# The second product of the last FFN: VectorE's emptying of a shared accumulator placed ahead of the splits, and two weight sums placed two steps later

## The chip, the core and the metric

The kernel runs on one core of one Trainium2 chip. A core has a matrix engine (TensorE, PE in the profile), which multiplies and adds into accumulators in PSUM, and three engines that work on vectors: VectorE (DVE), ScalarE (ACT) and GpSimd (POOL). Each engine carries out its own queue of instructions in order; semaphores let an instruction of one queue wait for another queue's. SyncE (SP) and GpSimd issue transfers here. The metric is the device time of one execution in microseconds (us), the median of several runs.

## The reference, cut to what matters

The program is a two-layer trunk over 512 tokens of width 1024, in float32. Each layer is a token mixer and a dense SwiGLU block, each with a norm before and after it. The change lies in the last SwiGLU block, in its second product (`@ w_out`, 512 x 2816 by 2816 x 1024), and so in the last 120 us of the program:

```python
def swiglu_ffn(h, w_in, w_out):
    gate, up = jnp.split(h @ w_in, 2, axis=-1)
    return (jax.nn.silu(gate) * up) @ w_out
...
        h = rmsnorm(x, norm_g[i, 2]) * (1.0 + scale) + shift
        y = swiglu_ffn(h, f_w_in[i], f_w_out[i])
        x = x + gate * rmsnorm(y, norm_g[i, 3])
```

## The kernel before

**Precision.** Every float32 operand of a matmul is split in two: ScalarE copies it into a rounded "high" half and VectorE subtracts that from the operand to get the "low" half. A product is then three matmuls: high by high, low weight by high, high by low activation (L1788). So every tile that TensorE reads has cost one ScalarE copy and one VectorE subtraction.

**Seven products in place of eight.** The 512 x 2816 activations and the 2816 x 1024 weights are cut into 2 x 2 blocks, and the four blocks of the result are made from seven block products (`PRODUCTS`), whose operands are sums and differences of blocks. The inner dimension is gone through in `NP` = 11 pairs `p` of 128-row blocks. Products 0 to 3 add into accumulators A, B, C and D; products 4, 5 and 6 add on into A. Each accumulator is two PSUM tiles, one for each half of 128 tokens: `bank["A"][0]` and `bank["A"][1]`, in the profile both `cA`.

**A is read three times on the way.** It is never restarted, so its value has to be taken out between products: after product 0 it is copied (the result block `got["11"]`, with B added later), after product 4 it is subtracted from C + D (`got["12"]`, L2018), after product 5 from D (`got["22"]`, L2020), and after product 6 it is the last block itself. TensorE may not add the next product's first step into a half of A before that half has been read.

**Parts.** The 77 steps (product, pair) are grouped into 40 parts of one or two steps. TensorE goes through them in order: the first token half of the part, then the second. A part of two steps is 12 matmuls, one of one step 6. Product 4 ends with part 27 (one step), product 5 is parts 28 to 33 (33 has one step), product 6 is parts 34 to 39.

**The order of the engines' queues** is the order of the code here: this stretch is recorded without the scheduler on all five engines. The loop over `n` (L2045) records, for each part, its matmuls (`products`), then the vector work due behind it (`behind`), then the splits of the weights of part n+4 (`w_prep`, L1754 on ScalarE and L1755 on VectorE, tile `whlo`, four buffers) and of the activations of part n+3 (`a_prep`, L1767 and L1768, tile `ao`, three buffers). Below, "w30" and "a29" are the splits for the weights of part 30 and the activations of part 29. With these buffer counts w30 waits for TensorE's part 26, and a29 for the same part. From part 34 on, `behind` comes after the splits.

**What `behind` does.** At n = 27 and 33 it empties A with two VectorE instructions, one per token half. At n = 29 and 30 ScalarE squares result blocks for the closing norm and VectorE forms a mean (L1983, L1986). From n = 34 on come the roots, the gates (L1993) and the sums into the output rows (L1999). `t3(p)` (L1801) is VectorE's weight sum for product 5: block 22 minus block 11 of pair p, in place. One is due at each n from 17 to 27; the sums of pairs 9 and 10, at n = 26 and 27, are read by ScalarE's copies w32 and w33.

Of the kernel before, what the change touches and what calls it, by code (L numbers as in the profile page):

```python
# [35 lines left out]
def trunk_kernel(  # L36
# [26 lines left out]
    def t2(name):  # L63
        return tmp.tile([P, T], F32, tag="t2", name=name, bufs=4)
# [985 lines left out]
    with ExitStack() as ph:  # L1050
# [99 lines left out]
        class Group:  # L1150
# [169 lines left out]
            def root(self):  # L1320
                self.rg = t2("rg")
                act.activation(self.rg, self.ssg, AF.Sqrt, bias=eps_t, scale=1.0 / 256)
# [219 lines left out]
    with ExitStack() as ph:  # L1542
# [4 lines left out]
        NP = NF // 2  # L1547
# [28 lines left out]
        def b_(i, name, q=None):  # L1576

            t = rows_of[i][int(name[1]) - 1][:, :, slice(0, T) if name[2] == "1" else slice(T, D)]
            return t if q is None else t[:, q, :]
# [156 lines left out]
        turns = [odd if i in (1, 3) else even for i in range(7)]  # L1736
# [7 lines left out]
        def w_prep(n):  # L1744
            w = whl_p.tile([P, 2, 2, T], F32R, tag="whl", name="whlo")
            part = parts[n]
            us = {unit_of[p] for _, p in part}
            if len(us) == 1 and len(part) == 2:
                todo = [(slice(0, 2), b_(us.pop(), PRODUCTS[part[0][0]][1]))]
            else:  # L1750
                todo = [(slice(q, q + 1), b_(unit_of[p], PRODUCTS[i][1])[:, units[unit_of[p]].index(p):][:, :1])
                        for q, (i, p) in enumerate(part)]
            for sl, srcw in todo:
                act.copy(w[:, 0, sl, :], srcw)  # L1754
                dve.tensor_tensor(w[:, 1, sl, :], srcw, w[:, 0, sl, :].bitcast(F32), SUB)  # L1755
            w_of[n] = w

        def a_prep(n):
            a = fo.tile([P, 2, 2, 256], F32R, tag="ao", name="ao")
            part = parts[n]  # L1760
            if len(part) == 2 and part[0][0] == part[1][0] and part[1][1] == part[0][1] + 1:
                todo = [(slice(0, 2), part[0], 2)]
            else:
                todo = [(slice(q, q + 1), st, 1) for q, st in enumerate(part)]
            for sl, (i, p), m in todo:
                srca = a_(PRODUCTS[i][2], p, m)
                act.copy(a[:, 0, sl, :], srca)  # L1767
                dve.tensor_tensor(a[:, 1, sl, :], srca, a[:, 0, sl, :].bitcast(F32), SUB)  # L1768
            for _, (i, p), m in todo:
                if i == 0:  # L1770
                    dve.tensor_tensor(a_("a11", p, m), a_("s1", p, m), a_("a11", p, m), SUB)
                elif i == 1:
                    dve.tensor_add(a_("a12", p, m), a_("a12", p, m), a_("a11", p, m))
            a_of[n] = a
# [3 lines left out]
        def products(tiles):  # L1778
            for sub in range(2):
                for n in tiles:  # L1780
                    for q, (i, p) in enumerate(parts[n]):
                        r = PRODUCTS[i][0]
                        if r not in bank:
                            bank[r] = [(mm_ps if r == "C" else aux_ps)(f"c{r}{t}") for t in range(2)]
                        first = i == {"A": 0, "B": 1, "C": 2, "D": 3}[r] and p == turns[i][0]
                        last = p == turns[i][-1]
                        w, a, tk = w_of[n], a_of[n], slice(sub * P, (sub + 1) * P)
                        for k, (hl, al) in enumerate(((0, 0), (1, 0), (0, 1))):  # L1788
                            pe.matmul(bank[r][sub], a[:, al, q, tk], w[:, hl, q, :],  # L1789
                                      start=first and k == 0, stop=last and k == 2, skip_group_check=True)  # L1790

        with tc.manual_schedule(engines={PE_ENGINE, mybir.EngineType.SP, mybir.EngineType.Activation,
# [5 lines left out]
            def t3(p):  # L1798
                i = unit_of[p]
                q = units[i].index(p)  # L1800
                dve.tensor_tensor(b_(i, "b11", q), b_(i, "b22", q), b_(i, "b11", q), SUB)  # L1801

            def t2_(i):
                add_(b_(i, "b22"), b_(i, "b12"))

            def t4(i):
                add_(b_(i, "b21"), b_(i, "b22"))
# [174 lines left out]
            def square(t, part, src):  # L1982
                act.activation(spare["junk"], src, AF.Square, accum_out=st[t]["s2"][:, part:part + 1])  # L1983

            def mean(t):
                dve.tensor_scalar(st[t]["b1"], st[t]["s2"][:, 0:1], 1.0 / D, EPS, MUL, ADD)  # L1986
# [5 lines left out]
            def gated(src, hf, dst):  # L1992
                dve.tensor_mul(dst, src, gg[hf])  # L1993
                return dst

            def x_new(t, hf, yg, parts=(FULL,), puts=(dma,)):
                for c, put in zip(parts, puts):
                    cx = slice(hf * T + c.start, hf * T + c.stop)
                    dve.scalar_tensor_tensor(xt[t][:, cx], yg[:, c], st[t]["s1"], xt[t][:, cx], MUL, ADD)  # L1999
                    put(out[0, t * P:(t + 1) * P, cx], xt[t][:, cx])  # L2000

            def behind(n):

                for t in range(2):
                    if n == 5:
                        got["11", t] = t2("c11")
                        act.copy(got["11", t], bank["A"][t])
                    elif n == 10:
                        dve.tensor_add(got["11", t], got["11", t], bank["B"][t])
                    elif n == 16:  # L2010
                        got["12", t] = t2("c12")
                        act.copy(got["12", t], bank["C"][t])
                    elif n == 21:
                        dve.tensor_add(got["12", t], got["12", t], bank["D"][t])
                        got["22", t] = spare[f"c22_{t}"]
                        act.copy(got["22", t], bank["D"][t])
                    elif n == 27:
                        dve.tensor_tensor(got["12", t], got["12", t], bank["A"][t], SUB)  # L2018
                    elif n == 33:
                        dve.tensor_tensor(got["22", t], got["22", t], bank["A"][t], SUB)  # L2020
                    elif n in (29, 30):
                        if t == n - 29:
                            square(t, 0, got["11", t])
                            square(t, 1, got["12", t])
                            mean(t)
                    elif n == 34:
                        root(t)
                        gated(got["11", t], 0, got["11", t])
                    elif n == 35:
                        square(2 + t, 0, got["22", t])  # L2030
                        mean(2 + t)
                        gated(got["12", t], 1, got["12", t])
                        x_new(t, 0, got["11", t])
                    elif n == 36:
                        gated(got["22", t], 1, got["22", t])
                        x_new(t, 1, got["12", t])
                for i, u in enumerate(units):
                    if n == 8 + u[-1] // 2:
                        t2_(i)
                    if n == 19 + i:  # L2040
                        t4(i)
                if 17 <= n < 17 + NP:
                    t3(turns[5][n - 17])

            for n in range(NT - 3):  # L2045
                products([n])
                if n < 34:
                    behind(n)
                if n == 26:
                    for hf in range(2):  # L2050
                        dma(gg[hf], gate_d[3, 4 * hf:4 * hf + 4].rearrange("j p -> (j p)").partition_broadcast(P))
                if n + 4 < NT:
                    w_prep(n + 4)
                if n + 3 < NT:
                    a_prep(n + 3)
                if n >= 34:
                    behind(n)
# [40 lines left out]
```

## Time and profile before

| what | us |
|---|---|
| median of 3 runs | 1345.12 |
| lowest, highest run | 1344.85, 1346.7 |
| the profiled execution's own time | 1345.17 |
| its span, first to last instruction | 1343.0 |
| TensorE idle between parts 27 and 28 | 2.02 |
| TensorE idle between parts 33 and 34 | 1.97 |
| TensorE idle ahead of part 39's last matmul of the first half | 0.39 |

The span is what the trace covers; the profiled execution's own time holds 2.2 us more around it. The parts of the changed stretch are read from the timeline, in us from the span's start: product 4 begins at 1286.26, product 5 at 1303.40, product 6 at 1320.60, and TensorE's last matmul ends at 1336.52. The mean granted TensorE clock is 0.999 of full speed. Matmuls overlap: the length of a group of them is not the sum of their single lengths. A wait is put down to one releaser, the one that came last by the profile.

### The profile page before, as it was taken

How to read it: one execution, taken by the hardware profiler on the slowest of the kernel's cores; microseconds unless marked ns; L12 is line 12 of the kernel's file. 1: busy time of each engine (PE TensorE's matmuls, PEld its weight loads, DVE VectorE, ACT ScalarE, POOL GpSimd, SP SyncE). 2: the span in 40 equal slices, each digit the busy share in tenths (PEclk: the TensorE clock that was granted, in tenths of full speed). 3: DMA queues.
4: the chain of work that ended last, by engine and by line, in shares of the span. 5: the costliest groups of instructions: out<-in, count | busy, mean ns of one | idle time of the engine just before them, and what ended most of it. 6: DMA issues, size and time to landing. Idle time of an engine off the chain costs nothing.

```text
span 1343.0 us, 19136 instructions
## 1 busy us (share of the span) xinstructions
PE 1326.6 (99%) x7485; PEld 1143.8 (85%) x7485; DVE 985.2 (73%) x1581; ACT 618.2 (46%) x995; POOL 65.3 (5%) x82
## 2 busy tenths in 40 slices
PE   8999999999999999999999999999999999999997
PEld 7788889888888888898888888888889999998875
DVE  5588866778787322659889988888677777767887
ACT  5323356222323211665644555554474555544664
POOL 0000000000000000000000000000000111101320
PEclk9999999999999999999999999999999999999999
DMA  9757760777776322513543344423251788779851
GB/s 311 237 179 233 252 206 1 225 245 234 238 247 221 126 94 67 157 33 118 165 130 114 91 128 124 132 73 125 79 157 46 192 219 210 199 200 286 166 108 63
DMA packets 199886, 215.90 MB, mean 161 GB/s; under 512 B 8292, under 2 KB 148468, under 8 KB 198772
## 3 DMA queue, kind: packets, MB, share of 16 engines
q1 hardware_dynamic: 186384, 184.74, 44.3%
q0 software_dynamic: 9264, 17.04, 7.4%
q10 hardware_dynamic: 4148, 12.90, 3.0%
q8 instruction: 59, 0.97, 0.3%
q14 instruction: 31, 0.25, 0.1%
HBM read 195.37 MB, written 2.24 MB: 147 GB/s over the span
## 4 chain that ended last, share of the span: by engine, by line
PE 91%; issue 3%; DMA 2%; ACT 2%; DVE 1%; SPq 0%; DVEq 0%; ACTq 0%; POOLq 0%
PE ip L276 14%; PE ip L278 14%; PE ip L277 14%; PE sA L1694 6%; PE y L378 6%; PE y L380 6%; PE y L379 6%; PE cA L1789 4%; PE sC L1694 3%; PE li L756 2%; PE li L276 2%; PE li L277 2%; PE li L278 2%; PE sB L1694 2%; PE yd L1283 1%
## 5 line engine op out<-in xcount | busy, mean ns | idle before, releaser
L276 PE MATMUL ip<-h,whl 128*128 128x512 f32 x840 | 331.2, 394 | 0.2 <-DVE cv L863 0.2
L278 PE MATMUL ip<-h,whl 128*128 128x512 f32 x840 | 327.2, 390 | 0.0
L277 PE MATMUL ip<-h,whl 128*128 128x512 f32 x840 | 327.0, 389 | 0.0
L276 PEld LDWEIGHTS ip<-h,whl 128*128 128x128 f32 x840 | 157.8, 188 | 33.8 <-issue 1.8
L278 PEld LDWEIGHTS ip<-h,whl 128*128 128x128 f32 x840 | 157.7, 188 | 33.4
L277 PEld LDWEIGHTS ip<-h,whl 128*128 128x128 f32 x840 | 157.8, 188 | 31.6
L222 DVE TENSOR_TENSOR whl<-wst,whl 128x1024 fp32r<-128x1024 f32 x99 | 120.4, 1221 | 60.1 <-ACT whl L221 59.9
L124 DVE SCALAR_TENSOR_TENSOR ada_acc<-ada_st,csil,ada_acc 128x512 f32<-128x512 f32 x140 | 105.0, 750 | 3.9 <-DMA ada_st<-in_ada_w_dram 0.4
L204 DVE TENSOR_TENSOR whlo<-wsto,whlo 128x1024 fp32r<-128x1024 f32 x41 | 49.9, 1224 | 78.2 <-ACT whlo L203 78.0
L221 ACT CAST whl<-wst 128x1024 fp32r<-128x1024 f32 x99 | 103.0, 1041 | 3.2 <-DMA wst<-in_a_w_in_dram 1.8
L276 PE MATMUL li<-h,whl 128*128 128x256 f32 x288 | 83.2, 289 | 0.0
L278 PE MATMUL li<-h,whl 128*128 128x256 f32 x288 | 81.6, 283 | 0.0
L277 PE MATMUL li<-h,whl 128*128 128x256 f32 x288 | 81.5, 283 | 0.0
L203 ACT CAST whlo<-wsto 128x1024 fp32r<-128x1024 f32 x41 | 42.6, 1050 | 76.4 <-PE y L380 75.0
L1694 PE MATMUL sA<-tq,whl 128*128 128x256 f32 x576 | 74.6, 283 | 0.3 <-DVE g L1720 0.3
L1694 PEld LDWEIGHTS sA<-tq,whl 128*128 128x128 f32 x576 | 71.6, 192 | 0.6 <-DVE g L1720 0.5
L378 PE MATMUL y<-whlo,ff 128*128 128x512 f32 x176 | 68.6, 390 | 0.0
L380 PE MATMUL y<-whlo,ff 128*128 128x512 f32 x176 | 68.5, 389 | 0.0
L379 PE MATMUL y<-whlo,ff 128*128 128x512 f32 x176 | 68.5, 389 | 0.0
L1142 DVE SCALAR_TENSOR_TENSOR cu<-ip,cols,cu 128x511 f32<-128x511 f32 (+2 forms) x84 | 62.8, 747 | 3.9 <-ACT cu L1139 1.4
L1789 PE MATMUL cA<-whlo,ao 128*128 128x512 f32 x264 | 61.2, 390 | 4.4 <-ACT ao L1767 4.0
L1789 PEld LDWEIGHTS cA<-whlo,ao 128*128 128x128 f32 x264 | 49.3, 188 | 15.7 <-ACT ao L1767 4.8
(328 smaller groups left out, 2436.0 us busy)
## 6 DMA issues: line engine op xcount, KB each, us to landing
ada_st<-in_ada_w_dram SPq DMA_DIRECT2D x96, 512.0 KB, 5.2
wst<-in_f_w_in_dram SPq DMA_DIRECT2D x26, 1024.0 KB, 6.5
wst<-in_m_w_in_dram SPq DMA_DIRECT2D x14, 1024.0 KB, 5.4
wsto<-in_f_w_out_dram SPq DMA_DIRECT2D x10, 1024.0 KB, 5.1
wst<-in_m_w_in_dram SPq DMA_DIRECT2D x20, 512.0 KB, 5.2
wst<-in_a_w_in_dram SPq DMA_DIRECT2D x9, 1024.0 KB, 5.9
wsu<-in_f_w_in_dram SPq DMA_DIRECT2D x17, 512.0 KB, 5.8
csb<-cs_d ACTq DMA_DIRECT2D x8, 1024.0 KB, 5.2
```

The source lines that it names most:

```text
L124: dve.scalar_tensor_tensor(acc, w, csil[:, k:k + 1], acc, MUL, ADD)
L221: later.append((lambda sw=sw, w=w: act.copy(w[:, 0, :nk, :], sw), lambda sw=sw, w=w: dve.tensor_tensor(w[:, 1, :nk, :], sw, w[:, 0, :nk, : ...
L222: lambda sw=sw, w=w: dve.tensor_tensor(w[:, 1, :nk, :], sw, w[:, 0, :nk, :].bitcast(F32), SUB)))
L276: pe.matmul(dst, w_at(w, 0, kk), a[:, 0, sl], start=start, stop=False)
L277: pe.matmul(dst, w_at(w, 0, kk), a[:, 1, sl], start=False, stop=False)
L278: pe.matmul(dst, w_at(w, 1, kk), a[:, 0, sl], start=False, stop=stop)
L378: pe.matmul(pst, a[:, 0, tk], wt[:, 0, kk, :], start=k == 0, stop=False)
L379: pe.matmul(pst, a[:, 0, tk], wt[:, 1, kk, :], start=False, stop=False)
L380: pe.matmul(pst, a[:, 1, tk], wt[:, 0, kk, :], start=False, stop=k == K - 1)
L1142: dve.scalar_tensor_tensor(u[:, sft:], pst[:, :T - sft], w[3 - sft], u[:, sft:], MUL, ADD)
L1694: pe.matmul(dst, w[:, wl, k0 + k, :], moving(q, k, al), skip_group_check=True, start=q in ("P1", "P5", "P2") and k == 0 and i == 0, stop=k ...
L1789: pe.matmul(bank[r][sub], a[:, al, q, tk], w[:, hl, q, :], start=first and k == 0, stop=last and k == 2, skip_group_check=True)
```

## The change

Two edits in the code that records this stretch.

- The loop no longer records part 27 in its own turn. At n = 26 it records part 26, its `behind`, then part 27 and `behind(27)`, and only then w30 and a29. In the same way parts 32 and 33 are recorded together, with `behind(33)` ahead of w36 and a35. TensorE's order of matmuls is the same as before.
- A table gives the weight sums that are due: none at n = 26 and 27, pair 9 at n = 28 and pair 10 at n = 29.

```diff
-                if 17 <= n < 17 + NP:
-                    t3(turns[5][n - 17])
+                for p in {26: (), 27: (), 28: (NP - 2,), 29: (NP - 1,)}.get(n, (n - 17,)):
+                    if 0 <= p < NP:
+                        t3(turns[5][p])
 
             for n in range(NT - 3):
-                products([n])
-                if n < 34:
+                if n not in (27, 33):
+                    products([n])
+                if n in (26, 32):
+                    behind(n)
+                    products([n + 1])
+                    behind(n + 1)
+                elif n < 34 and n not in (27, 33):
                     behind(n)
                 if n == 26:
```

VectorE's queue around the first emptying, as a piece of the difference. The first row is the low half of a28; L1801 is a weight sum, the three rows below the added pair are w30 (two) and a29, the rows at the end belong to w31:

```order
 L1768 TENSOR_TENSOR ao<-raw,ao 128x512
-L1801 TENSOR_TENSOR w2h_10839<-w2h_10840,w2h_10839 128x512
+L2018 TENSOR_TENSOR c_11258<-c_11258,cA_10902 128x512
+L2018 TENSOR_TENSOR c_11260<-c_11260,cA_10903 128x512
 L1755 TENSOR_TENSOR whlo<-w2t_10664,whlo 128x512
 L1755 TENSOR_TENSOR whlo<-w2s,whlo 128x512
 L1768 TENSOR_TENSOR ao<-raw,ao 128x512
-L2018 TENSOR_TENSOR c_11258<-c_11258,cA_10902 128x512
-L2018 TENSOR_TENSOR c_11260<-c_11260,cA_10903 128x512
-L1801 TENSOR_TENSOR w2h_10841<-w2h_10842,w2h_10841 128x512
 L1755 TENSOR_TENSOR whlo<-w2s,whlo 128x512
```

Four instructions that stood between a28 and the emptying stand behind it or further back, and the second sum leaves its place behind the emptying.

The two sums come back further down the same queue; the first row is a30's low half, then w32 (two), a31, a mean, w33:

```order
 L1768 TENSOR_TENSOR ao<-raw,ao 128x512
+L1801 TENSOR_TENSOR w2h_10839<-w2h_10840,w2h_10839 128x512
 L1755 TENSOR_TENSOR whlo<-w2h_10837,whlo 128x512
 L1755 TENSOR_TENSOR whlo<-w2h_10839,whlo 128x512
 L1768 TENSOR_TENSOR ao<-raw,ao 128x512
 L1986 TENSOR_SCALAR ss<-ss 128x1
+L1801 TENSOR_TENSOR w2h_10841<-w2h_10842,w2h_10841 128x512
 L1755 TENSOR_TENSOR whlo<-w2h_10841,whlo 128x512
```

Each sum now stands directly ahead of the splits that use its result (`w2h_10839` in w32, `w2h_10841` in w33).

VectorE's queue around the second emptying; the first two rows are w35 and a34, the rows after the added pair w36 (two) and a35, the last one w37:

```order
 L1755 TENSOR_TENSOR whlo<-w2t_10756,whlo 128x1024
 L1768 TENSOR_TENSOR ao<-raw,ao 128x512
+L2020 TENSOR_TENSOR w2h_10839<-w2h_10839,cA_10902 128x512
+L2020 TENSOR_TENSOR w2h_10841<-w2h_10841,cA_10903 128x512
 L1755 TENSOR_TENSOR whlo<-w2t_10664,whlo 128x512
 L1755 TENSOR_TENSOR whlo<-w2s,whlo 128x512
 L1768 TENSOR_TENSOR ao<-raw,ao 128x512
-L2020 TENSOR_TENSOR w2h_10839<-w2h_10839,cA_10902 128x512
-L2020 TENSOR_TENSOR w2h_10841<-w2h_10841,cA_10903 128x512
 L1755 TENSOR_TENSOR whlo<-w2s,whlo 128x512
```

Three splits that stood ahead of the pair stand behind it.

## The prediction

> **What bounds the kernel now.** I read the page's first part for the bound, then the list of waits for what TensorE (PE) waits for, then the timeline of each engine over the last 60 us, where the change lies. Columns of a timeline row: start in us, length in us, engine, line, operation, out<-in, count, and in brackets the idle time ahead of the row with what ended it.
>
> ```profile
> span 1343.0 us, 19136 instructions
> ...
> PE 1326.6 (99%) x7485; PEld 1143.8 (85%) x7485; DVE 985.2 (73%) x1581; ACT 618.2 (46%) x995; POOL 65.3 (5%) x82
> ...
> PE cA L1789 <- ACT ao L1767: 4.0, 2, 2.0
> ```
>
> TensorE is busy 99% of the span, so only its gaps can be won. The largest entry in its list of waits is the 4.0 us, in two waits, on the accumulator `cA` of the last product. They stand in TensorE's timeline:
>
> ```profile
> 1286.26 15.12 PE L1789 MATMUL cA<-whlo,ao 128*128 128x512 f32 x66
> 1303.40 15.22 PE L1789 MATMUL cA<-whlo,ao 128*128 128x512 f32 x66 [2.02 <-ACT ao L1767]
> 1320.60 11.61 PE L1789 MATMUL cA<-whlo,ao 128*128 128x512 f32 x50 [1.97 <-ACT ao L1767]
> 1332.60 3.92 PE L1789 MATMUL cA<-whlo,ao 128*128 128x512 f32 x16 [0.39 <-DVE ao L1768]
> ```
>
> Each x66 group is one product (11 pairs, 2 token halves, 3 matmuls), so a matmul is issued every (15.12-0.39)/65 = 0.227 us. TensorE stands still between parts 27 and 28 and between 33 and 34. The view blames a ScalarE copy into `ao`. VectorE (DVE) and ScalarE (ACT) at the first gap tell another story:
>
> ```profile
> 1298.42 1.23 DVE L1755 TENSOR_TENSOR whlo<-w2t,whlo 128x1024 fp32r<-128x1024 f32 x1 [0.56 <-ACT whlo L1754]
> 1299.57 0.69 DVE L1768 TENSOR_TENSOR ao<-raw,ao 128x512 fp32r<-128x512 f32 x1
> ...
> 1300.17 0.68 DVE L1801 TENSOR_TENSOR w2h<-w2h,w2h 128x512 f32<-128x512 f32 x1
> 1300.77 0.68 DVE L1755 TENSOR_TENSOR whlo<-w2t,whlo 128x512 fp32r<-128x512 f32 x1
> 1301.37 0.68 DVE L1755 TENSOR_TENSOR whlo<-w2s,whlo 128x512 fp32r<-128x512 f32 x1
> 1301.97 0.68 DVE L1768 TENSOR_TENSOR ao<-raw,ao 128x512 fp32r<-128x512 f32 x1
> 1302.58 1.28 DVE L2018 TENSOR_TENSOR c<-c,cA 128x512 f32<-128x512 f32 x2
> ...
> 1302.66 0.61 ACT L1767 CAST ao<-raw 128x512 fp32r<-128x512 f32 x1
> ```
>
> The `ao` copy at 1302.66 is the high half for part 30, which TensorE does not need for part 28. What part 28 needs is `cA` emptied: the first instruction of the L2018 pair ends at 1302.58+0.68 = 1303.26, and TensorE starts 0.14 us later, ahead of the pair's end at 1303.86: each token half is released by its own eviction. VectorE was never idle here. It did four instructions, 0.60 us apart, ahead of the eviction: a weight sum (L1801) and three splits for parts 30 and 29. The second gap has the same picture, without a sum:
>
> ```profile
> 1316.81 0.69 DVE L1768 TENSOR_TENSOR ao<-raw,ao 128x512 fp32r<-128x512 f32 x1
> ...
> 1317.96 0.69 DVE L1755 TENSOR_TENSOR whlo<-w2t,whlo 128x512 fp32r<-128x512 f32 x1 [0.46 <-ACT whlo L1754]
> ...
> 1319.78 1.28 DVE L2020 TENSOR_TENSOR w2h<-w2h,cA 128x512 f32<-128x512 f32 x2
> ```
>
> 1319.78+0.68+0.14 = 1320.60, TensorE's restart.
>
> **The first eviction moved.** Nothing is removed or added; VectorE's rows change places. With the sum and the splits gone from ahead of it, VectorE is free at 1300.17 and waits for the first half of `cA` alone. That this half is enough is seen at an earlier eviction, which began before the accumulator's last matmul ended (1286.42):
>
> ```profile
> 1271.98 14.44 PE L1789 MATMUL cD<-whlo,ao 128*128 128x512 f32 x63
> ...
> 1286.26 1.28 DVE L2014 TENSOR_TENSOR c<-c,cD 128x512 f32<-128x512 f32 x2
> ```
>
> Part 27 has six matmuls, three to a half. The half's last one is the first of these four:
>
> ```profile
> 1300.31 1.07 PE L1789 MATMUL cA<-whlo,ao 128*128 128x512 f32 x4
> ...
> 1317.33 1.29 PE L1789 MATMUL cA<-whlo,ao 128*128 128x512 f32 x5
> ```
>
> It ends at 1300.31+0.39 = 1300.70. How long VectorE takes to follow a matmul's end I bound by two rows: ScalarE follows TensorE's 1332.60+3.92 = 1336.52 at 1336.56 (0.04), and VectorE follows 1185.87+1.60 = 1187.47 at 1187.58 (0.11):
>
> ```profile
> 1185.87 1.60 PE L1694 MATMUL sB<-h,whl 128*128 128x256 f32 x12
> ...
> 1187.58 0.42 DVE L1707 TENSOR_TENSOR g<-sB,g 128x256 f32<-128x256 f32 x1 [1.05 <-PE sB L1694]
> ...
> 1336.56 0.60 ACT L1983 ACTIVATE w2s<-cA 128x512 f32<-128x512 f32 x1 [2.35 <-PE cA L1789]
> ```
>
> With 0.08: eviction at 1300.78, done at 1301.46, TensorE on at 1301.60 instead of 1303.40. **Gain 1.80** (1.77 to 1.84). A gap of 0.22 remains, since the last three matmuls of part 27 cover most of the eviction. The second half's eviction ends by 1302.2; TensorE reaches that half six matmuls (1.36) after 1301.60, at 1302.96.
>
> [...]
>
> **What is now late behind it.** The three splits come after both evictions: the low half of part 29's `ao` starts four places behind 1300.78, at about 1303.26, and is there at 1303.95 instead of 1302.65. TensorE wants it with the third matmul of part 29: 1301.60 + 2.72 (12 matmuls) + 0.45 = 1304.77, so 0.7 us of cover. If it were gone, a late split would cost TensorE its lateness once.
>
> **The two weight sums.** Each is 0.68 us on VectorE, not on TensorE's path, but ScalarE's copies for parts 32 and 33 read their results. Behind the evictions stand w30 (two), a29, w31 (two), a30, six at 0.60, so the first sum runs 1305.66 to 1306.34 and ScalarE's second w32 copy starts at 1306.38. Before, it began 0.52 into the first pair here (a mean, L1986, on VectorE stands among ScalarE's rows):
>
> ```profile
> 1306.42 1.14 ACT L1754 CAST whlo<-w2h 128x512 fp32r<-128x512 f32 x2 [3.15 <-PE cA L1789]
> ...
> 1307.99 0.63 ACT L1983 ACTIVATE w2s<-c 128x512 f32<-128x512 f32 x1
> ...
> 1308.74 0.63 ACT L1983 ACTIVATE w2s<-c 128x512 f32<-128x512 f32 x1
> 1308.90 0.14 DVE L1986 TENSOR_SCALAR ss<-ss 128x1 f32<-128x1 f32 x1
> ...
> 1311.86 1.05 ACT L1754 CAST whlo<-w2t 128x1024 fp32r<-128x1024 f32 x1
> ...
> 1314.58 1.05 ACT L1754 CAST whlo<-w2t 128x1024 fp32r<-128x1024 f32 x1 [1.36 <-PE cA L1789]
> ```
>
> Now I lay ScalarE out to the second gap: two copies (1.04), two squares at 0.75: free at 1308.92. The second sum stands on VectorE behind w32, a31 and a mean that needs the first square only: 1308.3 to 1309.0. So w33 at 1309.0, a32, two squares, w34 at 1311.56 (before 1311.86), a33, w35 at 1312.83 (its part-31 release moves to 1314.58-1.80 = 1312.78). VectorE follows: w34 at 1312.65, a33 1.14 later at 1313.8 (the step from 1298.42 to 1299.57), w35 at 1314.13 (0.34 for a narrow one, as from 1332.13 to 1332.47 in the rows of the tail below), a34 1315.27, free at 1315.87. The sums thus cost nothing as long as this is ahead of TensorE's half.
>
> **The second eviction moved.** Half 0 of part 33 ended at 1317.33+0.227+0.39 = 1317.94; 1.80 earlier is 1316.14, plus 0.08 is 1316.22, later than VectorE's 1315.87 by 0.35. Then 0.68 and 0.14: TensorE on at 1317.04 instead of 1320.60. **In all 3.56**, 1.76 from this place; bounds 3.50 to 3.64 by the lag.
>
> **Whether the end follows.** After part 34 the tail hangs on this chain: TensorE's part 34 frees ScalarE's buffer, then the table load, the roots, and VectorE down to part 39's last split, for which TensorE waits 0.39:
>
> ```profile
> 1323.64 1.14 ACT L1754 CAST whlo<-w2h 128x512 fp32r<-128x512 f32 x2 [3.11 <-PE cA L1789]
> ...
> 1325.32 1.28 ACT L1989 ACT_TABLE_LOAD   x1
> ...
> 1326.94 0.16 DVE L1990 RECIPROCAL ss<-ss 128x1 f32<-128x1 f32 x1 [0.75 <-ACT ss L1989]
> ...
> 1332.13 0.41 DVE L1768 TENSOR_TENSOR ao<-raw,ao 128x256 fp32r<-128x256 f32 x1
> 1332.47 0.68 DVE L1993 TENSOR_TENSOR w2h<-w2h,w2h 128x512 f32<-128x512 f32 x1
> ```
>
> All of it starts from part 34's end and moves with it, if VectorE has worked off its queue by the reciprocal: eleven instructions from 1316.22 at 0.60 end at 1322.9, the reciprocal's release is 1326.94-3.56 = 1323.38, so 0.5 us of cover. The 0.39 stays.
>
> The sum stands against the profiled execution, 1345.17 us, 0.05 above the median of 1345.12: 1345.1 - 3.56 = **1341.6 us**.
>
> **Rivals.** *VectorE late at the second place* (0.13): the sums make ScalarE and VectorE wait for each other twice, and my 0.35 of slack is thin. If the second sum had to wait for both squares, and the next mean too, w35 would be 1.5 late, the eviction 1.15: total 2.4, about 1342.7; half of that, 1342.1. For it: ScalarE ran without idle from 1306.42 to 1311.86. Against: the mean at 1308.90 waited for nothing, though the second square ran then.
>
> *The eviction waits for the whole part* (0.05): each starts 0.68 later, 2.2 in all, 1342.9. The L2014 row speaks against it.
>
> *The named releaser is right* (0.05): part 28 waits for ScalarE's `ao` copy, which stays at 1302.66; then nothing moves: 1345.1. For it: that copy ends within 0.02 of the first eviction's end, at both gaps. Against: it is another part's operand.
>
> *VectorE becomes the bound* (0.05), the one that ends slower: with its slack spent on waiting for `cA`, its three splits per part would no longer fit in TensorE's 2.72. At 0.60 they take 1.8; it decides from 0.91 per instruction. At the 1.14 of the wide splits (1298.42 to 1299.57) part 29 would wait 1.9 at each place, giving the gain back, and parts 30 to 33 0.7 each: +3, 1348. No 512-wide row here is near it. [...]
>
> **How the numbers follow.** The forecast, total 3.2 to 3.9, has 0.72. Its own range is 1341.1 to 1342.0, with about 0.3 for the spread of the runs. The upper end goes out over the late second place and the half-won case to 1343.4; the lower end, 1340.8, is both gaps gone (2.02+1.97 = 3.99) and 0.3. Left out are the last two rivals and a little more. A measurement of this kernel can tell about 0.2%, 2.7 us, from no change: faster is the forecast and a part of the first rival, 0.77; same, the rest of it and the next two, 0.18; slower 0.05.
>
> **What would show it.** In the changed profile L2018 should start near 1300.8 and L2020 near 1316.2, each ahead of the splits; TensorE's gaps should read about 0.2 and 0.2, the third still 0.39; ScalarE's w32 pair should be split by a wait on L1801. If L2018 starts past 1301.4, the half was not enough; if TensorE stays still until a row of ScalarE, the view's releaser was right. A second gap above 0.5 with L2020 right behind L1768 means VectorE was late. Gaps in front of parts 29 to 33 with VectorE busy throughout would make the prediction wrong in sign.

## The result and the profile after

| | before | changed |
|---|---|---|
| median of 5 runs, us | 1345.87 | 1341.62 |
| lowest, highest | 1344.85, 1346.7 | 1341.32, 1341.82 |
| the profiled execution's own time | 1345.17 | 1341.48 |
| its span | 1343.0 | 1339.4 |
| TensorE idle between parts 27 and 28 | 2.02 | 0.19 |
| TensorE idle between parts 33 and 34 | 1.97 | 0.19 |
| TensorE idle ahead of its last 16 matmuls | 0.39 | 0.39 |

The ratio of the times is 0.9966, with a 95% interval of 0.9954 to 0.9978. The forecast was 1341.6 in a range of 1340.8 to 1343.4. The two profiled executions differ by 3.69 us in time and 3.6 in span, against a forecast of 3.56. The medians differ by 4.25, because two more runs of the kernel before (1345.87 and 1346.55) moved its median up from the 1345.12 that the prediction started from; the last section says where the 0.7 between 4.25 and 3.56 most likely comes from.

The first lines of the changed kernel's page, and from its list of waits what TensorE's `cA` and the two emptyings wait for (us in total, times, longest):

```profile
span 1339.4 us, 19134 instructions
...
PE 1326.9 (99%) x7485; PEld 1144.0 (85%) x7485; DVE 984.7 (74%) x1581; ACT 617.9 (46%) x995; POOL 65.2 (5%) x82
```

```profile
DVE c L2018 <- PE cA L1789: 0.5, 1, 0.5
...
DVE w2h L2020 <- PE cA L1789: 0.3, 1, 0.3
...
PE cA L1789 <- DVE c L2018: 0.2, 1, 0.2
PE cA L1789 <- DVE w2h L2020: 0.2, 1, 0.2
```

The busy times are those of before to 0.5 us, and each engine has as many instructions: no work came or went, and the span is shorter by what TensorE no longer waits. The entry of 4.0 us on ScalarE's `ao` copy is gone. In its place stand two waits of 0.2 on VectorE's emptyings, and the emptyings now wait for TensorE, which they never did before: the direction of the wait has turned.

The timeline of the changed kernel, all three engines:

```profile
1300.75 1.37 DVE L2018 TENSOR_TENSOR c<-c,cA 128x512 f32<-128x512 f32 x2 [0.49 <-PE cA L1789]
...
1301.59 15.24 PE L1789 MATMUL cA<-whlo,ao 128*128 128x512 f32 x66 [0.19 <-DVE c L2018]
...
1302.68 0.62 ACT L1767 CAST ao<-raw 128x512 fp32r<-128x512 f32 x1
1303.24 0.68 DVE L1768 TENSOR_TENSOR ao<-raw,ao 128x512 fp32r<-128x512 f32 x1
...
1305.65 0.68 DVE L1801 TENSOR_TENSOR w2h<-w2h,w2h 128x512 f32<-128x512 f32 x1
...
1306.37 0.62 ACT L1754 CAST whlo<-w2h 128x512 fp32r<-128x512 f32 x1 [1.12 <-DVE w2h L1801]
...
1308.29 0.69 DVE L1801 TENSOR_TENSOR w2h<-w2h,w2h 128x512 f32<-128x512 f32 x1
...
1309.07 0.62 ACT L1754 CAST whlo<-w2h 128x512 fp32r<-128x512 f32 x1 [0.18 <-DVE w2h L1801]
...
1312.78 1.06 ACT L1754 CAST whlo<-w2t 128x1024 fp32r<-128x1024 f32 x1
...
1316.18 1.37 DVE L2020 TENSOR_TENSOR w2h<-w2h,cA 128x512 f32<-128x512 f32 x2 [0.33 <-PE cA L1789]
...
1317.02 11.61 PE L1789 MATMUL cA<-whlo,ao 128*128 128x512 f32 x50 [0.19 <-DVE w2h L2020]
...
1323.37 0.17 DVE L1990 RECIPROCAL ss<-ss 128x1 f32<-128x1 f32 x1 [0.40 <-ACT ss L1989]
...
1329.03 3.93 PE L1789 MATMUL cA<-whlo,ao 128*128 128x512 f32 x16 [0.39 <-DVE ao L1768]
```

The `ao` copy that the view of before named still runs at 1302.68, as at 1302.66 before, and TensorE went on at 1301.59 without it. L2018 starts 0.49 us after VectorE came free; TensorE resumes at 1301.59, which is 1300.75 + 0.68 + 0.16. The two sums stand at 1305.65 and 1308.29, and ScalarE waits for each. This costs nothing, for VectorE still waits 0.33 us ahead of L2020. From the restart at 1317.02 on, the distances are those of before: the last group of matmuls begins 12.01 later here (1329.03) and 12.00 later there (1332.60 - 1320.60). TensorE's last matmul ends at 1329.03 + 3.93 = 1332.96, which is 3.56 ahead of the 1336.52 of before.

### The profile page after: what moved, and what is told of

Read it like the earlier page. It is cut to its first block, busy times and chain, and to the rows that moved or that the text cites. A ratio compares the mean times of both kernels' runs of the same rounds, so it can differ in the third digit from the quotient of the medians.

```text
span 1339.4 us, 19134 instructions
## 1 busy us (share of the span) xinstructions
PE 1326.9 (99%) x7485; PEld 1144.0 (85%) x7485; DVE 984.7 (74%) x1581; ACT 617.9 (46%) x995; POOL 65.2 (5%) x82
## 4 chain that ended last, share of the span: by engine, by line
PE 95%; SPq 2%; DVE 1%; ACT 1%; DMA 1%; issue 0%; DVEq 0%; ACTq 0%
PE ip L276 14%; PE ip L278 14%; PE ip L277 14%; PE sA L1694 7%; PE y L378 6%; PE y L380 6%; PE y L379 6%; PE cA L1789 4%; PE sC L1694 3%; PE li L276 3%; PE li L278 3%; PE li L277 3%; PE sB L1694 2%; PE li L756 1%; PE yd L1283 1%; PE cD L1789 1%
```

## The experiments

All kernels were timed in five rounds against the kernel before, but for one that was profiled once. In each, TensorE's rows say where the time went.

### One place at a time, and the sums alone

Four kernels divide the change: only the first emptying ahead of the splits (with the sums as changed), only the second (with the sums at their old steps), both with the sums at their old steps, and the sums alone. The first, against the changed kernel; the second has 33 and 32 in place of 27 and 26, and both the second and the third have the lines below it:

```diff
-                if n not in (27, 33):
+                if n != 27:
                     products([n])
-                if n in (26, 32):
+                if n == 26:
...
-                elif n < 34 and n not in (27, 33):
+                elif n < 34 and n != 27:
                     behind(n)
```

```diff
-                for p in {26: (), 27: (), 28: (NP - 2,), 29: (NP - 1,)}.get(n, (n - 17,)):
-                    if 0 <= p < NP:
-                        t3(turns[5][p])
+                if 17 <= n < 17 + NP:
+                    t3(turns[5][n - 17])
```

The fourth, against the kernel before, has this edit the other way round and nothing else.

> Only parts 26 and 27 are recorded together (the first emptying ahead of w30 and a29); the second emptying stays behind w36 and a35; the sums stay where the change put them. Theory (each place is worth its own 1.8 us): TensorE's first gap 0.2, the second 2.0 as before, about 1.8 us below before and 1.8 above the change, near 1343.4. Rival (the second gap closes by itself once VectorE runs earlier): both gaps small, near 1341.6. Rival (what is won first is given back at the second place): second gap near 3.7, no gain.

> Only parts 32 and 33 are recorded together; the first emptying and both sums stand as in the kernel before. Theory: first gap 2.0, second 0.2, 1.8 us below before, near 1343.4. Rival (the second place needs the sums' move or the first place): the second gap stays above 1.

> Both emptyings moved, the two weight sums at their old steps (one ahead of the first emptying, one right behind it). Theory: VectorE idled 0.49 ahead of the first emptying in the change, and one sum takes 0.60, so L2018 starts only 0.03 to 0.1 later; the other sum makes a29 0.6 later, inside its 0.7 of cover. Time as the change, 1341.6, at most 0.2 above. Rival (the sums had to move): each costs its 0.6 on TensorE's path, 1342.2 to 1342.8, with a gap in front of part 29.

> Only the two weight sums two steps later, both emptyings where they were. Theory: the splits ahead of the first emptying then wait for ScalarE's copies, which end at 1300.68 and after, so L2018 starts at most 0.05 earlier: time as before. Rival (each instruction ahead of the emptying costs its 0.6): 0.6 below before, first gap 1.4.

| kernel | median, us | runs | ratio to before, 95% interval |
|---|---|---|---|
| first place alone | 1344.47 | 11 | 0.9979 to 0.9997 |
| second place alone | 1344.47 | 11 | 0.9978 to 0.9996 |
| both, sums at their old steps | 1341.39 | 5 | 0.9952 to 0.9977 |
| the sums alone | 1345.21 | 11 | 0.9986 to 1.0003 |

The first two were expected near 1343.4, and their medians lie 1.1 above that. Their profiled executions took 1343.30 and 1343.76 us; the runs of each fall into two groups, one at 1343.1 to 1343.8 and one at 1344.2 to 1345.7. The gaps below are those of the shorter group, and the last experiments look at the longer one.

TensorE in the timeline, first place alone, then second place alone:

```profile
1301.59 15.24 PE L1789 MATMUL cA<-whlo,ao 128*128 128x512 f32 x66 [0.19 <-DVE c L2018]
1318.80 11.61 PE L1789 MATMUL cA<-whlo,ao 128*128 128x512 f32 x50 [1.97 <-ACT ao L1767]
```

```profile
1303.86 15.24 PE L1789 MATMUL cA<-whlo,ao 128*128 128x512 f32 x66 [2.02 <-ACT ao L1767]
1319.29 11.61 PE L1789 MATMUL cA<-whlo,ao 128*128 128x512 f32 x50 [0.19 <-DVE w2h L2020]
```

Each edit takes away its own gap and leaves the other untouched: the two places do not depend on each other, and in the trace the gain is their sum. Both with the sums at their old steps, TensorE and the two emptyings:

```profile
1300.48 1.34 DVE L2018 TENSOR_TENSOR c<-c,cA 128x512 f32<-128x512 f32 x2
...
1301.31 15.24 PE L1789 MATMUL cA<-whlo,ao 128*128 128x512 f32 x66 [0.22 <-DVE c L2018]
...
1315.91 1.37 DVE L2020 TENSOR_TENSOR w2h<-w2h,cA 128x512 f32<-128x512 f32 x2 [0.49 <-PE cA L1789]
...
1316.74 11.62 PE L1789 MATMUL cA<-whlo,ao 128*128 128x512 f32 x50 [0.19 <-DVE w2h L2020]
```

With a sum ahead of it, L2018 starts as soon as VectorE is free and not when TensorE is done, and the first gap is 0.22 in place of 0.19. VectorE is then 0.49 early at the second place, where the changed kernel is 0.33 early. So moving the sums buys 0.03 us at the first place and uses up 0.16 us of slack at the second; in the time neither shows (1341.15 to 1341.67 here, 1341.32 to 1341.82 for the change). The sums alone left both gaps as they were. Without the first sum the split behind it waited 0.46 us for ScalarE's copy, so taking this one instruction away freed next to nothing:

```profile
1300.99 0.69 DVE L1755 TENSOR_TENSOR whlo<-w2t,whlo 128x512 fp32r<-128x512 f32 x1 [0.46 <-ACT whlo L1754]
...
1303.63 15.20 PE L1789 MATMUL cA<-whlo,ao 128*128 128x512 f32 x66 [1.98 <-ACT ao L1767]
1320.81 11.61 PE L1789 MATMUL cA<-whlo,ao 128*128 128x512 f32 x50 [1.97 <-ACT ao L1767]
```

### Is a half released by its own emptying?

The prediction read this off two coincidences in time. The test empties the second half first:

```diff
                     elif n == 27:
-                        dve.tensor_tensor(got["12", t], got["12", t], bank["A"][t], SUB)
+                        dve.tensor_tensor(got["12", 1 - t], got["12", 1 - t], bank["A"][1 - t], SUB)
                     elif n == 33:
-                        dve.tensor_tensor(got["22", t], got["22", t], bank["A"][t], SUB)
+                        dve.tensor_tensor(got["22", 1 - t], got["22", 1 - t], bank["A"][1 - t], SUB)
```

> The changed kernel, but at both places VectorE empties the second token half before the first. Theory (TensorE goes on with a token half as soon as that half of the accumulator is empty, 0.14 us behind VectorE): the emptying of the second half cannot start before the last matmul of the part (1301.39 in the changed kernel's profile, with 0.05 for the start), takes 0.68, the first half takes 0.68 behind it, and TensorE's next part begins with the first half: gap 0.05 + 0.68 + 0.68 + 0.14 = 1.55 in place of 0.19, at both places, so 1341.62 + 2 x 1.36 = 1344.3 us. Rival 1 (the tile order within a pair does not matter because TensorE is released by both emptyings or by the whole part): both gaps stay at 0.19 and the time at 1341.6. Rival 2 (a gap well over 1 us also brings the second cluster of times seen where a 2 us gap is left): as the theory, with part of the runs 1.2 to 1.6 above the rest.

Measured: 1344.09 us (11 runs, 1343.73 to 1344.65; ratio 0.9979 to 0.9997). The timeline of this kernel:

```profile
1302.10 1.28 DVE L2018 TENSOR_TENSOR c<-c,cA 128x512 f32<-128x512 f32 x2 [1.17 <-PE cA L1789]
...
1303.53 15.21 PE L1789 MATMUL cA<-whlo,ao 128*128 128x512 f32 x66 [1.47 <-ACT whlo L1754]
```

VectorE waits 1.17 us, now for the end of the whole part. TensorE waits for both emptyings, since the half that it wants comes second: 1302.10 + 1.28 = 1303.38, and it starts 0.15 later. In the changed kernel it went on at 1301.59, ahead of the pair's end at 1300.75 + 1.37 = 1302.12. The two kernels together show that an emptying waits for its own half, and a half's matmuls for their own emptying. The gap is 1.47 at both places: reversing two instructions at each gives back 2 x (1.47 - 0.19) = 2.56 us of the 3.61 by which the change had shortened the two gaps. The row again names a ScalarE copy, this time of a `whlo` tile: the view's releaser is whatever ended last, and here it was wrong in another way than before.

### How much room is there, ahead of the emptying and behind it?

Three VectorE subtractions on operands that nobody needs any more, once ahead of the second emptying, once behind the first:

```diff
                     products([n + 1])
+                    if n == 32:
+                        for _ in range(3):
+                            dve.tensor_tensor(a_("a12", 0, 2), a_("a12", 0, 2), a_("a12", 0, 2), SUB)
                     behind(n + 1)
```

```diff
                     behind(n + 1)
+                    if n == 26:
+                        for _ in range(3):
+                            dve.tensor_tensor(a_("a12", 0, 2), a_("a12", 0, 2), a_("a12", 0, 2), SUB)
```

> The changed kernel with three more 128x512 VectorE subtractions (on operands that are dead by then, 0.60 us from one to the next) directly ahead of the emptying at the second place. Theory (VectorE was free at 1315.85 and waited 0.33 us for TensorE there; past that every hundredth of VectorE's work ahead of the emptying is paid in full): 3 x 0.60 - 0.33 = 1.47 us, gap between parts 33 and 34 of 0.19 + 1.47 = 1.66, time 1343.1 us, and the first place unchanged at 0.19. Rival 1 (VectorE has more room, the emptying is held by something else): less than 1 us. Rival 2 (the gap of 1.66 brings the second cluster of times): low runs at 1343.1, others 1.2 to 1.6 above.

> The changed kernel with the same three VectorE subtractions directly behind the emptying at the first place, so ahead of the low half of the split w30 and of the split a29's, which the change had put behind the emptying. Theory (the splits behind the emptying have about 0.7 us of cover before TensorE's part 29 needs them): L2018 and gap 27/28 unchanged (0.19), a new gap of about 1.8 - 0.7 = 1.1 us ahead of part 29 that ends on the low half of a29, second place at most some tenths later, time 1342.7 to 1343.1 us. Rival (the splits have several us of cover, so their place behind the emptying costs nothing in any amount): no new gap, 1341.6.

Ahead: 1343.43 us (11 runs, 1342.73 to 1344.91; ratio 0.9977 to 0.9995). Behind: 1343.30 us (11 runs, 1342.86 to 1344.74; 0.9973 to 0.9991). The timeline of the kernel with three ahead, then that with three behind:

```profile
1315.81 2.14 DVE L2054 TENSOR_TENSOR raw<-raw 128x512 f32<-128x512 f32 x3
...
1317.87 1.28 DVE L2020 TENSOR_TENSOR w2h<-w2h,cA 128x512 f32<-128x512 f32 x2
...
1318.70 11.61 PE L1789 MATMUL cA<-whlo,ao 128*128 128x512 f32 x50 [1.83 <-DVE w2h L2020]
```

```profile
1301.37 3.46 PE L1789 MATMUL cA<-whlo,ao 128*128 128x512 f32 x14 [0.19 <-DVE c L2018]
1305.82 12.12 PE L1789 MATMUL cA<-whlo,ao 128*128 128x512 f32 x52 [1.00 <-DVE ao L1768]
...
1317.62 1.27 DVE L2020 TENSOR_TENSOR w2h<-w2h,cA 128x512 f32<-128x512 f32 x2
...
1318.44 11.58 PE L1789 MATMUL cA<-whlo,ao 128*128 128x512 f32 x50 [0.50 <-DVE w2h L2020]
```

The three take 1317.87 - 1315.81 = 2.06 us, not the 1.80 assumed. Ahead of the emptying 1.64 of it is paid (1.83 - 0.19), so the room there is 0.42. Behind the emptying TensorE stops at part 29, whose `ao` is late. The bracket there reads 1.00, but it counts from the end that the profile gives the matmul before, and inside a run of matmuls, which are 0.39 us long and start every 0.227, the next one starts ahead of that end. What is paid shows from restart to restart: 1318.44 - 1301.37 = 17.07 us in place of the changed kernel's 1317.02 - 1301.59 = 15.43, so 1.64 more (the medians differ by 1.68). Of this, 0.31 (0.50 - 0.19) falls to the second emptying, 12 us on, where L2020 has no wait left. The other 1.33 falls to part 29: the room there is 2.06 - 1.33 = 0.73, and the splits' place behind the emptying is free only up to that.

### The rest of each gap

What was left of each gap is the first half's emptying, less the three matmuls of the second half that cover it. Run together, parts 26 and 27 give it nine:

```diff
                 if n not in (27, 33):
-                    products([n])
+                    products([n, n + 1] if n in (26, 32) else [n])
                 if n in (26, 32):
                     behind(n)
-                    products([n + 1])
                     behind(n + 1)
```

> The changed kernel, but TensorE runs parts 26 and 27 (and 32 and 33) as one: the first token half of both, then the second half of both, so the first half's accumulator is complete 9 matmuls (1.93 us) ahead of the end in place of 3 (0.64). Theory (what is left of each gap, 0.19, is the 0.68 + 0.05 + 0.14 of the first half's emptying less 0.64 of TensorE's second half): the first half is empty before TensorE needs it, both gaps vanish, 1341.62 - 0.38 = 1341.24 us; VectorE's emptying of the first half then starts right behind the split of a28 (and a34) with no wait for TensorE. Rival (0.19 is the cost of any hand-over between accumulator contents, hidden or not): gaps and time stay, 1341.6.

Measured: 1341.15 us (5 runs, 1340.71 to 1341.53; ratio 0.9954 to 0.9979), 0.47 below the change by the medians, and 0.38 was expected. The medians alone do not show this step: they come from different sets, and the changed kernel's interval is 0.9954 to 0.9978. The trace does. Its timeline:

```profile
1285.96 41.91 PE L1789 MATMUL cA<-whlo,ao 128*128 128x512 f32 x182
...
1299.87 0.68 DVE L2018 TENSOR_TENSOR c<-c,cA 128x512 f32<-128x512 f32 x1
...
1301.12 0.69 DVE L2018 TENSOR_TENSOR c<-c,cA 128x512 f32<-128x512 f32 x1 [0.57 <-PE cA L1789]
...
1328.26 3.92 PE L1789 MATMUL cA<-whlo,ao 128*128 128x512 f32 x16 [0.40 <-DVE ao L1768]
```

182 matmuls in one row: TensorE passes both emptyings without a gap. The first half's emptying no longer waits, the second half's alone does. From the start of product 4 to the end of TensorE's last matmul it takes 1328.26 + 3.92 - 1285.96 = 46.22 us, where the changed kernel, whose product 4 starts at 1286.27, takes 1332.96 - 1286.27 = 46.69. A hand-over of the accumulator costs nothing once it is covered: 0.19 us with three matmuls of cover, no gap with nine.

One gap is left, ahead of the last 16 matmuls. To this kernel one more edit was added, the last split three VectorE instructions earlier:

```diff
                 for t in range(2):
+                    if n == 35 and t == 1:
+                        a_prep(39)
...
-                if n + 3 < NT:
+                if n + 3 < NT and n != 36:
                     a_prep(n + 3)
-                if n >= 34:
+                if n == 36:
+                    behind(35)
+                if n in (34, 36):
                     behind(n)
```

> The kernel with parts 26 and 27, and 32 and 33, run at once (1341.15 us in its first runs), and the low half of the last split, a39's, three VectorE instructions earlier (ahead of the second token half's mean, gate and sum of step 35 in place of behind them). Theory (the last gap of TensorE, 0.40 ahead of its last 16 matmuls, ends with that split, and VectorE, which then has no idle time up to the first half's last gate, is the other limit of the tail): TensorE's gap goes, the last matmul ends 0.40 earlier, but VectorE's own queue ahead of the gate keeps its length, so the end comes 0.1 to 0.3 earlier: 1340.9 to 1341.1 us. Rival 1 (the end follows TensorE alone): the full 0.40, 1340.75. Rival 2 (VectorE's queue alone sets the end): no gain, 1341.15.

Measured: 1341.17 us (5 runs, 1340.96 to 1341.45; ratio 0.9952 to 0.9979), no change that the times could show. Its timeline, with VectorE's last row:

```profile
1286.31 45.56 PE L1789 MATMUL cA<-whlo,ao 128*128 128x512 f32 x198
...
1334.61 0.88 DVE L1999 SCALAR_TENSOR_TENSOR x<-yg,ss,x 128x256 f32<-128x256 f32 x2
```

In the kernel without this edit, VectorE's last row is this:

```profile
1334.40 0.88 DVE L1999 SCALAR_TENSOR_TENSOR x<-yg,ss,x 128x256 f32<-128x256 f32 x2
```

Counted from the start of product 4, TensorE's last matmul ends after 45.56 us in place of 46.22, but VectorE's last instruction after 1334.61 + 0.88 - 1286.31 = 49.18 in place of 49.32. Of 0.66 us won on TensorE (again more than the bracket's 0.40) 0.14 arrives. VectorE's queue of gates and sums has no idle time there and became the limit of the tail: the chain of work that ended last holds TensorE's 16 matmuls, 3.93 us, without this edit, and from the table load on no matmul with it. Removing the largest gap that is left is worth next to nothing.

### What a gap of TensorE does to its clock

The kernels that keep a gap of some 2 us had runs in two groups, the changed kernel in one. Six of the dead subtractions ahead of the second emptying (`range(6)` in the diff above) make a longer gap.

> The changed kernel with six of the dead VectorE subtractions directly ahead of the emptying at the second place (three took 2.06 us, so 0.69 each). Time without any effect on the clock: gap 0.19 + 6 x 0.69 - 0.33 = 4.0 us, 1341.5 + 3.8 = 1345.3 us, one cluster of runs. Theory on the second cluster of times (kernels with a gap of TensorE of 1.8 to 2.0 us had 38 of 87 runs some 1.2 to 1.6 us longer, at a mean granted clock lower by 0.001, kernels with gaps up to 0.22 none of 15: an idle stretch of TensorE lowers the granted clock for a while, depending on where it falls): a gap of 4.0 does it in nearly all runs, the stretch behind the gap shows a granted clock well under 1.00, and the time is 1346.5 to 1347.2 us. Rival (the second cluster comes from transfers or another cause outside these gaps): the granted clock stays 1.00 behind the gap and the share of long runs stays below a half, median 1345.3.

Measured: 1347.44 us (11 runs, 1346.64 to 1348.51; ratio 1.0002 to 1.002). No run lay near the 1345.3 that the gap alone would give; the median is even above the 1346.5 to 1347.2 that was expected. TensorE in the timeline of this kernel, then the table of stretches (TensorE's busy us and matmuls, granted clock, DMA):

```profile
1321.60 14.31 PE L1789 MATMUL cA<-whlo,ao 128*128 128x512 f32 x50 [4.00 <-DVE w2h L2020]
```

```profile
1320.00:1321.00 1.00, 0.00 (x0) 0.76 0.00 0
1321.00:1322.00 1.00, 0.40 (x1) 0.50 0.00 0
...
1326.00:1327.00 1.00, 1.00 (x4) 0.50 0.00 0
1327.00:1328.00 1.00, 1.00 (x5) 0.83 0.00 0
1328.00:1330.00 2.00, 2.00 (x10) 1.00 0.00 0
```

The granted clock is 0.50 from about 1320.5 to 1327.3, and the 50 matmuls behind the gap take 14.31 us in place of 11.61. To see the same behind a gap of 2 us, the kernel with the first place alone changed was run twice more.

> The kernel with the first place alone changed, once more, for a profile of a longer execution (8 of its 11 runs lay between 1344.2 and 1345.7 us, 3 at 1343.2). Theory (the gap of 1.97 us between parts 33 and 34 lowers the granted clock for a while in most runs): if the profiled run is a longer one, the matmuls behind that gap run at a granted clock under 1.00 and the parts behind it take some 1.2 to 1.6 us longer than the 11.61 us and 3.93 us in the first profile. Rival (the extra time lies ahead of the last feed-forward, the start of its stretch in the profile moves): the stretch of parts 22 to 27 starts 1.2 to 1.6 us later and the rest is as before. If the profiled run is a short one, neither is told.

> The kernel with the first place alone changed, a third time, for a profile of one of its longer executions. The run with six operations ahead showed the clock at 0.50 for 6.8 us behind a gap of 4.0 us. Theory (a gap of 1.97 us does the same for about half as long, when it falls so): if the profiled run lies at 1344.2 us or above, the granted clock behind the gap between parts 33 and 34 is 0.50 for about 2.4 to 3.4 us and the 50 matmuls behind it take 1.2 to 1.6 us longer than 11.61. Rival (the longer executions lose their time elsewhere): the clock stays 1.00 there and the stretch before part 22 is longer. In either case about two thirds of the runs are expected at 1344.2 to 1345.7 us, the others at 1343.0 to 1343.3.

The first of these was one execution at 1343.05 us, a short one, with a granted clock of 0.999 over the whole, and told nothing. The second gave a median of 1344.54 (11 runs, 1342.93 to 1344.96; ratio 0.9978 to 0.9996), and its profiled execution was a long one, 1344.8 us. TensorE in its timeline, then its stretches:

```profile
1318.75 13.21 PE L1789 MATMUL cA<-whlo,ao 128*128 128x512 f32 x50 [1.97 <-ACT ao L1767]
```

```profile
1318.00:1319.00 1.00, 0.25 (x1) 1.00 0.00 0
1319.00:1320.00 1.00, 1.00 (x5) 0.74 0.00 0
1320.00:1321.00 1.00, 1.00 (x4) 0.50 0.00 0
...
1322.00:1323.00 1.00, 1.00 (x4) 0.56 0.00 0
1323.00:1324.00 1.00, 1.00 (x6) 1.00 0.00 0
```

The same kernel's short execution, its first profile, has 1.00 in the same place:

```profile
1320.00:1321.00 1.00, 1.00 (x6) 1.00 0.00 0
```

The gap is 1.97 us in both. In the long execution TensorE comes back at full clock, drops to 0.50 some 0.7 us later (about 1319.5, since the stretch from 1319 has 0.74 in the mean) and stays there for about 3.4 us; the 50 matmuls take 13.21 us where the short one has 11.61 (quoted above), 1.60 more. Everything ahead of the gap is the same (product 5 starts at 1301.53 and 1301.59), so the rival, a loss ahead of this stretch, is out for this execution.

## Why the prediction was right, step by step

**What TensorE waited for.** Right. The named `ao` copy stayed where it was and TensorE went on 1.1 us ahead of it. Reversing the two emptyings showed the link from the other side: TensorE followed the emptying of the half it needed, 0.15 us behind its end.

**The first place.** L2018 was forecast at 1300.78 and TensorE at 1301.60; they stood at 1300.75 and 1301.59. The gain by the gap is 2.02 - 0.19 = 1.83 against 1.80, and alone this place took exactly its own gap away. The lag of VectorE behind TensorE, bounded by 0.04 and 0.11, was about 0.05 in place of the 0.08 assumed, and TensorE's own lag behind the emptying 0.16 in place of 0.14; the two small errors cancel in part.

**What is late behind it.** The low half of part 29's `ao` came at 1303.24, forecast 1303.26, and made no gap. The 0.7 us of cover was right: 0.73 by the three operations behind the emptying. The price given for lateness past it, paid once, was too low: of 2.06 us 1.33 was paid at part 29 and 0.31 again at the second place.

**The two sums.** Right: forecast 1305.66 and 1308.3, measured 1305.65 and 1308.29; w33 at 1309.07 against 1309.0, w35 at 1312.78 against 1312.83. The experiment with the sums at their old steps shows that this edit was not needed for the gain.

**The second place.** L2020 was forecast at 1316.22 and stood at 1316.18, TensorE at 1317.02 against 1317.04. The slack of VectorE, the weak point, was put at 0.35; the profile has 0.33 and the three operations ahead put it at 0.42.

**The tail.** The third gap stayed at 0.39, and the reciprocal came at 1323.37 against 1323.38. VectorE had waited 0.40 us there for ScalarE's root, where 0.5 of cover was forecast.

**The rivals.** VectorE late at the second place: it was 0.33 early. The emptying waits for the whole part: it would have started at 1301.4 and started at 1300.75. VectorE becomes the bound: its splits kept their step of 0.60 and no gap appeared in parts 29 to 33.

**What the sum did not contain.** It priced a gap at its length alone. The medians differ by 0.7 us more than that, most likely because a gap of 2 us sometimes costs clock as well; this is shown on one execution of another kernel (1.60 us there) and inferred for the kernel before.

**What was luck.** The mechanism and the places are borne out, each by its own row. That the median fell within 0.02 us of the forecast is closer than the sum could promise: its own range was 1341.1 to 1342.0, and the five runs spread over 0.5.

## What to carry to other kernels

When the view names a releaser, ask which operand the waiting instruction needs, and see which instruction on that operand ended 0.1 to 0.2 us ahead of the restart: here the named engine was wrong by coincidence at both gaps. In an engine that works in order (VectorE here: three operations on other operands ahead of L2020 held TensorE up by 1.64 us), put the instruction that frees a shared accumulator ahead of the preparation for later parts, and in the order in which the halves are wanted, up to the cover that this preparation has (0.7 us here). A gap of the matrix engine can cost more than its length (1.97 us of idle time and 1.60 of slower matmuls in one execution here), so look at the spread of the runs and at the granted clock behind it, and expect the end to follow another engine once the last gaps are gone (of 0.66 us won on TensorE 0.14 arrived here).

## What was not expected of the hardware

**A gap of 2 us can cost 3.6.** In the long execution above, the second gap cost 1.97 us of idle time and 1.60 of slower matmuls. Over all sets, the kernel before ran 89 times: 53 runs lie at 1344.71 to 1346.05 us (median 1345.21) and 36 at 1346.26 to 1348.27 (median 1346.82), 1.61 apart. The kernel with the first place alone changed has 8 of 23 runs at 1342.9 to 1343.5 and 15 at 1344.2 to 1345.7. The changed kernel and the three others whose gaps here are 0.4 us at most never had a second group in 20 runs, and with the 4.0 us gap all 11 runs were long. The shorter group of before less the changed kernel's median is 1345.21 - 1341.62 = 3.59, close to the forecast's 3.56. Two of the first five runs of before were long, so the median of those five is the slowest of the three short ones, and that is the rest of the 4.25. That the long runs of the kernel before are the same thing is inferred: the size is equal (1.61 and 1.60), and in the 84 of its runs that list a mean granted clock all 50 shorter ones have 0.999 and all 34 longer ones 0.997 or 0.998. Its one profile is of a short execution.

The half clock lasts about 3.4 us in the execution with the 1.97 us gap (1319.5 to 1322.9) and about 6.8 in the one with the 4.0 us gap (1320.5 to 1327.3, the first 1.1 us of it still in the gap), that is once and twice the same length. What sets this length, and why only some executions are hit, no run here shows. In the long execution 1.97 us was enough, inside a stretch whose rest was busy (15.81 of the 16 us from 1300 to 1316).

**Where it begins is open.** The kernels with one gap of 2 us had more long runs (15 of 23 and 6 of 11) than those with two (36 of 89 for the kernel before, 4 of 11 with the sums alone), which a fixed chance for each gap would not give. With a gap of 1.83 us (three operations ahead) 5 of 11 runs were at 1344.5 to 1344.9 and the others at 1342.7 to 1343.4. With two gaps of 1.47 us the 11 runs spread from 1343.73 to 1344.65 without a second group. With gaps of 1.00 and 0.50 us two of 11 runs were at 1344.6 to 1344.7, over a microsecond above most others, which a threshold on the length of one gap does not explain; no profile of such a run was taken.

**Operations in place on one operand followed each other more slowly.** Three subtractions that read and write one operand took 2.06 us, 0.69 each, where others of this size on VectorE stood 0.60 apart. What makes them slower was not tested.
